# Padding of the low operand tile in the far SBUF pool: 40 elements instead of 8

## The chip, the cores and the metric

The kernel runs on one core of one Trainium2 chip. The metric is the device time of one execution in microseconds, as the median of several. Before the change three executions took 2014.45 to 2016.31 us, with a median of 2016.3 us.

## What is computed

One layer of an encoder trunk in float32, for one sequence of 256 tokens of width 2048. The normalised input goes through one wide projection that feeds three mixers (chunked attention, a diagonal state-space model called S5, and an mLSTM) and their gates; the gated sum is projected and added to the input; then come a cross-attention to 256 memory tokens and a gated feed-forward of width 5632:

```python
h = _rms(x, norm_mix[i])
qa, ka, va, us, xm, vm, om, im, fm, gpre = jnp.split(h @ w_in[i], splits, axis=-1)
...
merged = (gates[:, :, 0] * (ya @ w_br_a[i])
          + gates[:, :, 1] * (ys @ w_br_s[i])
          + gates[:, :, 2] * (ym @ w_br_m[i]))
x = x + merged @ w_out[i]
x = x + _mem_attention(_rms(x, norm_x[i]), mem_n, w_xq[i], w_xkv[i], g_xq[i], g_xk[i], w_xo[i])
x = x + _swiglu(_rms(x, norm_ffn[i]), w_gu[i], w_down[i])
```

## The kernel before

**Split products.** Every large product is made of three. Each float32 operand is split into a high part, rounded to the format that TensorE takes in one pass (`F32R`), and a low part, what is left. A product is high by high, plus high by low, plus low by high, added up in PSUM. `split_w` (lines 111 to 118) splits a weight block: ScalarE copies it into `whi` (line 116), VectorE subtracts into `wlo` (line 117). `split_act` (lines 203 to 210) does the same with an activation.

**The wide product, `gemm_i`** (lines 120 to 155). For 512 output columns it goes through the depth in tiles of 128 and through the two halves of the tokens. The activations, transposed so that depth lies along the partitions, are the stationary operand (128x128, loaded anew for each matmul); the weights stream past as the moving operand (128x512). There are three matmuls a step:

```python
PE.matmul(o, sh, h, start=(kt == 0), stop=False)              # line 146: high x whi
PE.matmul(o, sh, lw, start=False, stop=False)                 # line 147: high x wlo
PE.matmul(o, xl[:, kt, t * P:(t + 1) * P], h, start=False,    # line 148: low x whi
```

So a product of depth 2048 and 512 columns is 96 matmuls. `gemm_ii` (lines 157 to 175) is the other way about: the weights are stationary, the activations stream with 256 columns (lines 169 to 171).

**The operands.** An operand is a pair of tiles, high and low, of 16 depth tiles by 256 tokens, 16,384 bytes a partition each. Each stage writes the operand of the next: `to_operand` (lines 821 to 835) transposes four blocks on TensorE (line 827) and splits them. The stages that follow one another in time, with their stationary operands:

- the input projection: `xT` in poolA; within it the branch products with `ym`, `ya` and `ys` in p1, and the S5 gate, `gemm_ii` with `yg` in s5
- `w_out` (lines 880 to 889): `mT` in poolB, four products, 384 matmuls
- `w_xkv` (lines 915 to 937): `eT` in poolA, eight products, 768 matmuls
- `w_xq` (lines 946 to 997): `x1T` in poolB, four products, 384 matmuls, broken up by the attention of each head
- `w_xo` (lines 1001 to 1006): `oT` in poolA, 384 matmuls
- `w_gu` (lines 1016 to 1028): `x2T` in poolB, eleven rounds of a gate and an up product, 2112 matmuls, with eight transposes a round
- `w_down` (lines 1030 to 1039): `hT` in p3, four products of depth 5632, 1056 matmuls

**Where they lie.** The pools wp, poolA, p1 and s5 (later p2 and p3) are stacked upwards from the low end of SBUF, in the order in which they are opened. poolB and px1 are on the right side: poolB is stacked down from byte 229,344 of the partition and px1, with the residual `x1`, lies below it. Within a pool the tiles lie in the order of their first use. `mT`, `x1T` and `x2T` follow one another in the same two tiles of poolB. The byte offsets in a partition, worked out from the tiles' sizes and the allocator's order, before the change:

| tile | bytes from | modulo 256 |
|---|---|---|
| whi, wlo (four buffers each) | 36,672 to 65,344, every 4,096 | 64 |
| xT, eT, oT, high and low | 88,896 and 105,280 | 64 |
| hT, high and low | 88,896 and 133,952 | 64 |
| ya | 139,072 | 64 |
| ym, ys | 164,608 | 0 |
| yg | 198,528 | 128 |
| gt (two buffers) | 84,416 and 86,464 | 192 |
| part | 122,688 and on, every 4,096 | 64 |
| x1 | 180,160 | 192 |
| mT, x1T, x2T, high | 196,544 | 192 |
| mT, x1T, x2T, low | 212,928 | 192 |

All slices of an operand start at multiples of 512 bytes within it, so all lie at the same place modulo 256.

**What sets the order.** The scheduler orders the instructions by priority; weight loads and their splits come first (`WPRI`), PSUM evictions second (`EPRI`). Weights come in blocks of 1 MB through SyncE's queue (line 101), two buffers deep. The matmuls keep the order of the program, with transposes and the attention's small products put in between.

Of the kernel before, what the change touches and what calls it, by code (L numbers as in the profile page):

```python
# [10 lines left out]
F32R = mybir.dt.float32r  # L11
# [7 lines left out]
P = 128  # L19
T = 256  # L20
D = 2048
KD = D // P
# [30 lines left out]
def tile_block(ctx: ExitStack, tc: tile.TileContext, a: dict, out: bass.AP):  # L53
# [758 lines left out]
    poolB = tc.alloc_tile_pool(name="poolB", bufs=1, side="right")  # L812

    def operand_low(name):

        t = poolB.tile([P, KD * T + 8], F32R, tag="Bl", name=name)
        return t[:, 0:KD * T].rearrange("p (k t) -> p k t", t=T)
    mTh = poolB.tile([P, KD, T], F32R, tag="Bh", name="mT_h")
    mTl = operand_low("mT_l")

    def to_operand(srcs, dh, dl, k0, gname=None):
# [104 lines left out]

    fTh = poolB.tile([P, KD, T], F32R, tag="Bh", name="x1T_h")
    fTl = operand_low("x1T_l")
    for n in range(4):
        to_operand([x1[:, t, n * 512:(n + 1) * 512] for t in range(2)], fTh, fTl, 4 * n, "norm_x")  # L930
# [67 lines left out]

    gTh = poolB.tile([P, KD, T], F32R, tag="Bh", name="x2T_h")
    gTl = operand_low("x2T_l")  # L1000
    off = 0
    for n in range(4):
# [148 lines left out]
```

## Time and profile before

| | |
|---|---|
| profiled execution | 2013.28 us |
| its span | 2011.5 us |
| TensorE busy, matmuls | 2000.9 us, 9880 matmuls |
| TensorE busy, weight loads | 1670.1 us |
| VectorE busy | 1249.9 us |
| ScalarE busy | 975.0 us |
| GpSimd busy | 78.6 us |
| DMA | 377.78 MB, mean 188 GB/s |

The profile shows one execution. In a group of instructions by line the columns are the line, the engine, the operation, the output and the inputs by their names, the shape, the count, and then the busy time, the mean duration in ns and the idle time before. Matmuls overlap: each starts before the one ahead has ended, and their ends are modelled. So the pace of TensorE is the distance from one start to the next, which is read from the timeline (columns: start in us, duration in us, engine, line, operation, operands, count).

### The profile page before, as it was taken

The page shows a single profiled execution, that of the slowest core. Times are in us where ns is not written, and L with a number is a line of the kernel's source. Part 1 is how long each engine was busy: PE and PEld are TensorE (multiplying, and loading weights), DVE is VectorE, ACT ScalarE, POOL GpSimd, SP SyncE. Part 2 cuts the span into 40 slices and gives each one's busy share as a digit, 9 for nine tenths or more (in the row PEclk, how much of TensorE's full clock was granted, in tenths as well). Part 3 has the DMA queues.
Part 4 walks back from the last instruction along what each step waited for, and adds up shares of the span by engine and source line. Part 5 has one row for each costly group of instructions (what it writes and reads, how often), then busy time and mean ns, then how long its engine had stood idle before and what let it go on. Part 6 is the DMA issues. An engine that isn't in the chain of part 4 may idle for free.

```text
span 2011.5 us, 25145 instructions
## 1 busy us (share of the span) xinstructions
PE 2000.9 (99%) x9880; PEld 1670.1 (83%) x9880; DVE 1249.9 (62%) x1804; ACT 975.0 (48%) x1332; POOL 78.6 (4%) x142
## 2 busy tenths in 40 slices
PE   9999999999999999999999999999999999999999
PEld 7998888887887888888888888888888888888887
DVE  7967896669987857554545656554544444444443
ACT  7555556555444455555545545444444444433332
POOL 1001202000000000011000000000000000000000
PEclk9999999999999999999999999999999999999999
DMA  8555355555555656755454435555555555555553
GB/s 312 180 178 178 134 172 196 171 186 177 194 175 196 209 186 225 257 205 188 168 192 174 157 134 181 188 188 188 173 185 187 188 188 181 179 190 210 204 199 136
DMA packets 60406, 377.78 MB, mean 188 GB/s; under 512 B 6912, under 2 KB 8064, under 8 KB 18816
## 3 DMA queue, kind: packets, MB, share of 16 engines
q1 hardware_dynamic: 56880, 367.42, 52.0%
q0 software_dynamic: 2112, 6.82, 1.4%
q8 instruction: 77, 1.26, 0.3%
q10 hardware_dynamic: 1296, 1.95, 0.3%
q14 instruction: 41, 0.34, 0.0%
HBM read 374.06 MB, written 2.10 MB: 187 GB/s over the span
## 4 chain that ended last, share of the span: by engine, by line
PE 93%; DVE 4%; DMA 2%; ACT 0%; issue 0%; POOL 0%; SPq 0%; DVEq 0%; ACTq 0%
PE acc L147 27%; PE acc L146 27%; PE acc L148 27%; PE acc L170 2%; PE acc L169 2%; PE acc L171 2%; DVE wlo L117 2%; DMA raw<-in_w_in_dram 2%; PE sm L827 1%; PE sm L993 1%; PE sm L967 1%; PE sm L411 1%; ACT whi L116 0%; DVE s2k L442 0%; PE sm L911 0%
## 5 line engine op out<-in xcount | busy, mean ns | idle before, releaser
L117 DVE TENSOR_TENSOR wlo<-raw,whi 128x1024 fp32r<-128x1024 f32 (+2 forms) x700 | 833.9, 1193 | 668.2 <-ACT whi L116 665.0
L116 ACT CAST whi<-raw 128x1024 fp32r<-128x1024 f32 (+2 forms) x700 | 715.0, 1027 | 883.9 <-PE acc L148 677.1
L146 PE MATMUL acc<-whi,x2T_h 128*128 128x512 f32 x704 | 279.0, 396 | 0.0
L147 PE MATMUL acc<-wlo,x2T_h 128*128 128x512 f32 x704 | 278.9, 396 | 0.0
L148 PE MATMUL acc<-whi,x2T_l 128*128 128x512 f32 x704 | 278.0, 395 | 0.0
L147 PE MATMUL acc<-wlo,xT_h 128*128 128x512 f32 (+2 forms) x704 | 262.3, 373 | 1.8 <-DVE wlo L117 1.6
L148 PE MATMUL acc<-whi,xT_l 128*128 128x512 f32 (+2 forms) x704 | 261.1, 372 | 0.0
L146 PE MATMUL acc<-whi,xT_h 128*128 128x512 f32 (+2 forms) x704 | 259.7, 373 | 0.3 <-ACT whi L116 0.3
L148 PEld LDWEIGHTS acc<-whi,x2T_l 128*128 128x128 f32 x704 | 132.2, 188 | 31.7
L146 PEld LDWEIGHTS acc<-whi,x2T_h 128*128 128x128 f32 x704 | 132.2, 188 | 31.5
L147 PEld LDWEIGHTS acc<-wlo,x2T_h 128*128 128x128 f32 x704 | 132.2, 188 | 31.5
L147 PEld LDWEIGHTS acc<-wlo,xT_h 128*128 128x128 f32 x704 | 132.4, 188 | 27.3 <-DVE wlo L117 4.4
L146 PEld LDWEIGHTS acc<-whi,xT_h 128*128 128x128 f32 x704 | 131.8, 188 | 24.8 <-issue 1.3
L148 PEld LDWEIGHTS acc<-whi,xT_l 128*128 128x128 f32 x704 | 132.4, 188 | 23.3 <-issue 0.7
L147 PE MATMUL acc<-wlo,hT_h 128*128 128x512 f32 x352 | 137.0, 389 | 0.0
L146 PE MATMUL acc<-whi,hT_h 128*128 128x512 f32 x352 | 137.0, 389 | 0.0
L148 PE MATMUL acc<-whi,hT_l 128*128 128x512 f32 x352 | 136.9, 389 | 0.0
L169 PE MATMUL acc<-xT_h,whi 128*128 128x256 f32 x352 | 100.3, 285 | 2.1 <-DVE ev L627 2.1
L170 PE MATMUL acc<-xT_l,whi 128*128 128x256 f32 x352 | 100.7, 286 | 0.0
L148 PE MATMUL acc<-whi,eT_l 128*128 128x512 f32 x256 | 100.2, 391 | 0.0
L147 PE MATMUL acc<-wlo,eT_h 128*128 128x512 f32 x256 | 99.9, 390 | 0.0
L146 PE MATMUL acc<-whi,eT_h 128*128 128x512 f32 x256 | 99.8, 390 | 0.0
(376 smaller groups left out, 2832.3 us busy)
## 6 DMA issues: line engine op xcount, KB each, us to landing
raw<-in_w_gu_dram SPq DMA_DIRECT2D x88, 1024.0 KB, 4.7
raw<-in_w_in_dram SPq DMA_DIRECT2D x68, 1024.0 KB, 4.8
raw<-in_w_down_dram SPq DMA_DIRECT2D x44, 1024.0 KB, 4.7
raw<-in_w_xkv_dram SPq DMA_DIRECT2D x32, 1024.0 KB, 4.7
raw<-in_w_ii_dram SPq DMA_DIRECT2D x22, 1024.0 KB, 4.9
raw<-in_w_out_dram SPq DMA_DIRECT2D x16, 1024.0 KB, 5.0
raw<-in_w_xq_dram SPq DMA_DIRECT2D x16, 1024.0 KB, 4.7
raw<-in_w_xo_dram SPq DMA_DIRECT2D x16, 1024.0 KB, 4.7
```

Of the source, the lines that this page charges most:

```text
L116: S.copy(hi[:, :n], raw[:, c0:c1])
L117: V.tensor_tensor(lo[:, :n], raw[:, c0:c1], hi[:, :n].bitcast(F32), ALU.subtract)
L146: PE.matmul(o, sh, h, start=(kt == 0), stop=False)
L147: PE.matmul(o, sh, lw, start=False, stop=False)
L148: PE.matmul(o, xl[:, kt, t * P:(t + 1) * P], h, start=False, stop=(kt == nk - 1))
L169: PE.matmul(po, h, xh[:, kt, :], start=(kt == 0), stop=False)
L170: PE.matmul(po, h, xl[:, kt, :], start=False, stop=False)
L171: PE.matmul(po, lo[:, j * P:(j + 1) * P], xh[:, kt, :], start=False, stop=(kt == nk - 1))
L411: PE.matmul(pb[e][:, i * T:(i + 1) * T], bT[q:q + 32, i, c, :], u[q:q + 32, c, :], start=True, stop=True, tile_position=(q, 0))
L827: PE.transpose(px[:, j * T + t * P:j * T + (t + 1) * P], srcs[t][:, (kp + j) * P:(kp + j + 1) * P], ident)
L967: PE.matmul(pS[:, t * T:(t + 1) * T], qx[:, qi, d, t * P:(t + 1) * P], kx[:, ki, d], start=(d + i == 0), stop=(d == 3 and i == 2))
L993: PE.matmul(po[:, j * T:(j + 1) * T], vx[:, vi, m, c0:c0 + P], pT[pi][:, m * T:(m + 1) * T], start=(m + i == 0), stop=(m == 1 and i == 2))
```

## The change

One number, in the function that makes the low tile of an operand in poolB:

```diff
     def operand_low(name):
 
-        t = poolB.tile([P, KD * T + 8], F32R, tag="Bl", name=name)
+        t = poolB.tile([P, KD * T + 40], F32R, tag="Bl", name=name)
         return t[:, 0:KD * T].rearrange("p (k t) -> p k t", t=T)
     mTh = poolB.tile([P, KD, T], F32R, tag="Bh", name="mT_h")
     mTl = operand_low("mT_l")
```

The tile has KD x T = 4096 elements of four bytes and a padding that nothing reads or writes; the padding grows from 32 to 160 bytes. What is computed stays the same.

## The prediction

> **What bounds the kernel now.** I read the page first, then the chain of waits, then the matmuls one by one. On the page only the first lines matter.
>
> ```profile
> span 2011.5 us, 25145 instructions
> ...
> PE 2000.9 (99%) x9880; PEld 1670.1 (83%) x9880; DVE 1249.9 (62%) x1804; ACT 975.0 (48%) x1332; POOL 78.6 (4%) x142
> ...
> PE 93%; DVE 4%; DMA 2%; ACT 0%; issue 0%; POOL 0%; SPq 0%; DVEq 0%; ACTq 0%
> ```
>
> TensorE is busy all the time and is 93% of the chain that ends last. From 783 us to 2005 us, where all that the change touches lies, the chain by line names PE alone. What a matmul takes there is what the kernel takes. The chain, in order of time, gives a ruler for the gate and up stage: the six transposes of line 827 come once in each of its eleven rounds.
>
> ```profile
> 1269.93 0.65 PE sm L827 x6
> ...
> 1772.09 0.65 PE sm L827 x6
> ```
>
> So a round (192 matmuls and eight transposes) lasts (1772.09 - 1269.93) / 11 = 45.65 us.
>
> Now the matmuls. All that I compare are of the same form, 128x128 stationary against 128x512 moving, from lines 146 to 148. Busy means are no measure here, as each matmul begins before the last has ended. Their order in the groups by form is still telling:
>
> ```profile
> L146 PE MATMUL acc<-whi,x2T_h 128*128 128x512 f32 x704 | 279.0, 396 | 0.0
> ...
> L146 PE MATMUL acc<-whi,hT_h 128*128 128x512 f32 x352 | 137.0, 389 | 0.0
> ...
> L146 PE MATMUL acc<-whi,x1T_h 128*128 128x512 f32 x128 | 50.6, 395 | 0.0
> L146 PE MATMUL acc<-whi,mT_h 128*128 128x512 f32 x128 | 50.5, 395 | 0.0
> ...
> L146 PE MATMUL acc<-whi,oT_h 128*128 128x512 f32 x128 | 49.4, 392 | 0.0
> ```
>
> The three operands of the far pool (x2T, x1T, mT) stand at 395 and 396 ns, the others at 389 to 392. To get the true step I took the timeline of PE, with the starts of the first and the last matmul of a stretch, two rows for each operand, picked out of the answers for the windows in which they stand. The steps between them: x2T 190, hT 1033, mT 348, eT 121, x1T 121, ym 47, ya 47.
>
> ```profile
> 1270.34 0.47 PE L147 MATMUL acc<-wlo,x2T_h 128*128 128x512 f32 x1
> 1314.74 0.39 PE L148 MATMUL acc<-whi,x2T_l 128*128 128x512 f32 x1
> 1772.50 0.48 PE L147 MATMUL acc<-wlo,hT_h 128*128 128x512 f32 x1
> 2006.75 0.39 PE L148 MATMUL acc<-whi,hT_l 128*128 128x512 f32 x1
> 794.41 0.48 PE L148 MATMUL acc<-whi,mT_l 128*128 128x512 f32 x1
> 875.36 0.40 PE L148 MATMUL acc<-whi,mT_l 128*128 128x512 f32 x1
> 875.60 0.39 PE L146 MATMUL acc<-whi,eT_h 128*128 128x512 f32 x1
> 903.03 0.40 PE L147 MATMUL acc<-wlo,eT_h 128*128 128x512 f32 x1
> 1056.98 0.40 PE L146 MATMUL acc<-whi,x1T_h 128*128 128x512 f32 x1
> 1085.11 0.39 PE L147 MATMUL acc<-wlo,x1T_h 128*128 128x512 f32 x1
> 462.25 0.62 PE L146 MATMUL acc<-whi,ym 128*128 128x512 f32 x2
> 473.01 0.39 PE L148 MATMUL acc<-whi,ym 128*128 128x512 f32 x1
> 566.53 0.39 PE L146 MATMUL acc<-whi,ya 128*128 128x512 f32 x1
> 577.18 0.39 PE L148 MATMUL acc<-whi,ya 128*128 128x512 f32 x1
> ```
>
> Time over steps: eT 27.43 / 121 = 226.7 ns, ya 10.65 / 47 = 226.6, hT 234.25 / 1033 = 226.8; ym 10.76 / 47 = 228.9; x1T 28.13 / 121 = 232.5, mT 80.95 / 348 = 232.6, x2T 44.40 / 190 = 233.7. Put the addresses beside them. The moving operands whi and wlo always lie at 64 modulo 256. The stationary operands at 64 (eT, ya, hT, in three pools) step at 226.7; the one at 0 (ym) at 228.9; those at 192 (the far pool) at 232.5 to 233.7. One form, three phases, three paces; and the clock is the same, as the rows by stage further down show it at 1.00 for mT, x2T and hT alike.
>
> **The change, part by part.** Padding of 40 instead of 8 elements makes the low tile 16,544 bytes instead of 16,416. The pool is stacked down from byte 229,344, so the low tile goes from 212,928 to 212,800, the high tile from 196,544 to 196,416, and x1 below them from 180,160 to 180,032. All three go from 192 to 64 modulo 256. No instruction is added or removed, none is resized, and nothing is queued elsewhere.
>
> *Gate and up, 2112 matmuls on x2T.* The stretch of 44.40 us has 190 steps, the first of them long (it follows transposes; its row shows 0.47 us). The hT stretch begins the same way: 234.25 us less 1033 steps at eT's 226.69 ns leaves 0.08 us for that. At phase 64 the x2T stretch would take 190 x 0.22669 + 0.08 = 43.15 us: 1.25 us less, 6.58 ns a step. Over 2112 matmuls: 13.9 us. *w_out, 384 on mT.* 80.95 against 348 x 0.22669 + 0.08 = 78.97: 1.98 us, 5.7 ns a step; over 384: 2.2 us. *Cross-attention queries, 384 on x1T.* 28.13 against eT's 27.43 over 121 steps each: 5.8 ns; over 384: 2.2 us. Together 18.3 us.
>
> From this something comes off. After a break by other matmuls the pace has to settle again. The oT stage, at phase 64 but broken up by attention heads, shows 392 ns where hT shows 389: 3 ns a matmul. The x1T stage is broken up in the same way, so I take 384 x 3 ns = 1.1 us off: **17.2 us**. If mT pays this too, it is 18.3 - 2.3 = 16.0; if neither does, 18.3.
>
> Three edits come at nothing. x1 moves too: TensorE reads it in transposes alone, and these take the same 272 ns from x at 192 and from part at 64:
>
> ```profile
> L827 PE MATMUL sm<-cc,x 128*128 128x128 f32 x64 | 8.8, 272 | 0.0
> ...
> L827 PE MATMUL sm<-cc,part 128*128 128x128 f32 x32 | 4.6, 272 | 0.0
> ```
>
> The new lower edge of the pool lies within tiles of the S5 stage on which its old edge lay; the low tile now touches one more S5 scratch slot, for which the high tile waits already. And x1's edge stays 1,024 bytes above vx and hT_l, which end at 179,008. So no wait is added. If one were, it would hold up the splits of ACT and DVE into the operand, and the matmuls of w_out behind them, once.
>
> Does another engine become late when PE goes 3% faster? The stages of mT, x2T and hT side by side (time, then PE, PEld, DVE, ACT, POOL busy with counts, clock, DMA share, GB/s):
>
> ```profile
> 785.00:875.00 90.00, 90.00 (x393) 73.05 (x392) 53.75 (x64) 47.47 (x71) 3.98 (x8) 1.00 0.73 254
> 1264.00:1766.00 502.00, 502.00 (x2201) 405.08 (x2200) 244.67 (x225) 212.40 (x227) 1.46 (x4) 1.00 0.52 184
> 1767.00:2007.00 240.00, 240.00 (x1064) 198.60 (x1062) 110.49 (x97) 90.48 (x87) 0.00 (x0) 1.00 0.53 187
> ```
>
> The hT stage already runs the same weight loads and splits at the fast pace, with DVE and ACT under half busy and DMA at 0.53. The mT stage has DMA at 0.73, which becomes 0.75. Neither is a bound, so PE's time comes off the end one for one.
>
> The profiled execution took 2013.28 us, 1.8 over its span; less 17.2 that is 1996.1. It lies 3.0 us under the median of 2016.3 of the runs shown, so the median forecast is 2016.3 - 17.2 = **1999.1 us**.
>
> **A rule that speaks against it.** Rows first: same form, same clock, 226.7 ns at phase 64 and 233.7 at phase 192. The Trainium skill, "TensorE: Matmul & The Clock Gate", "Step-by-step: what each phase is for", says that TensorE has two independent read ports, and that loading the next weights takes no read bandwidth from the running matmul. By that rule an address could not matter and the sum would be 0, at 2016.3. The trace does not agree: something between the weight load and the stream depends on where they lie.
>
> **The rivals.** *The place, not the phase.* All three slow operands lie above byte 196,000, and no fast one of this form does. If the far end itself is slow, or the pool isn't stacked as I worked out, nothing changes: 2016.3. For it: place and phase can't be told apart for these three. Against it: ym is at 164,608, far below, and is off the fast pace too, at 228.9; hT runs at one pace over 90 KB of addresses; and yg, moving operand of the narrow matmuls, lies at 198,528 and is not slow (next rival). I give it 8%.
>
> *A middling pace.* mT and x2T lie at the same bytes, yet step at 232.6 and 233.7, so history has a hand in it. The new place might settle at ym's 228.9, 2.2 above the fast pace: (6.58 - 2.2) x 2112 + (5.75 - 2.2) x 768 = 9.3 + 2.7 = 12.0 us, 2004.3. Against it: eT, ya and hT all settle at the same value. 7%.
>
> *Like phases collide, so it gets slower.* In the narrow matmuls (lines 169 to 171, 256 columns, weights stationary at 64) it seems to be so. Two rows each, 251 and 107 steps:
>
> ```profile
> 60.43 0.36 PE L170 MATMUL acc<-xT_l,whi 128*128 128x256 f32 x1
> 90.63 0.28 PE L169 MATMUL acc<-xT_h,whi 128*128 128x256 f32 x1
> 737.10 0.28 PE L169 MATMUL acc<-yg,whi 128*128 128x256 f32 x1
> 749.71 0.28 PE L171 MATMUL acc<-yg,wlo 128*128 128x256 f32 x1
> ```
>
> With xT at 64, like the weights, a step takes 30.20 / 251 = 120.3 ns; with yg at 128, 12.61 / 107 = 117.9. Like phases cost 2.4 ns there. Were that so for wide matmuls at the far end, twice the columns would make it 4.9 ns, 14.1 us over 2880 matmuls: 2030.4. It decides if the wide pace at like phases is above 233.7. Against it stand eT, ya and hT, wide and alike, at 226.7. 3%.
>
> **How the numbers follow.** The forecast gets 82%, the rivals 8, 7 and 3%. A measurement of this kernel can tell about 0.2%, 4 us, from no change. The forecast and the middling pace are faster by more: 0.89; the place 0.08 same; collision 0.03 slower. The forecast's own bounds, savings of 16.0 to 18.3, give 1998.0 to 2000.3; the runs shown scatter from 2014.45 to 2016.31 and the profiled one is at 2013.28, so 3 us go under it: 1995.0. At the top the range reaches past the middling pace: 2005.0. Left out are the place and the collision and little else.
>
> **What would show it.** Right: in the profile after, starts on x2T, mT and x1T step at 226.7 to 227.5 ns; mean durations of x2T come down from 396 to about 389; a gate and up round on the chain lasts 45.65 - 192 x 6.58 ns = 44.4 us; PE stays at 99%. Wrong: steps still at 232 to 234 (the place), at 229 (middling), above 234 (collision); or the steps fall and PE waits for whi or wlo instead.

## The result and the profile after

The median went from 2015.64 us (four runs, 2014.45 to 2016.31) to 1997.24 us (four runs, 1997.08 to 1997.32): 18.4 us less, a ratio of 0.9909 with a 95% interval of 0.9892 to 0.9926. The profiled executions stand at 2013.28 and 1997.28 us, 16.0 apart. The instructions and their order on each engine are the same.

The page after the change, the same lines as before:

```profile
span 1995.5 us, 25145 instructions
...
PE 1984.5 (99%) x9880; PEld 1670.1 (84%) x9880; DVE 1249.9 (63%) x1804; ACT 976.4 (49%) x1332; POOL 77.8 (4%) x142
```

TensorE is still busy 99% of a span that is 16 us shorter, and its busy time has gone down by 16.4 us with the same 9880 matmuls. This is not a wait removed: the matmuls follow one another at a shorter distance. The ruler on the chain, the transposes that come once a round of gate and up:

```profile
1267.33 0.66 PE sm L827 x6
...
1756.06 0.66 PE sm L827 x6
```

A round lasts (1756.06 - 1267.33) / 11 = 44.43 us, against 45.65. The groups by form show which matmuls it was:

```profile
L146 PE MATMUL acc<-whi,x2T_h 128*128 128x512 f32 x704 | 274.9, 391 | 0.0
...
L146 PE MATMUL acc<-whi,hT_h 128*128 128x512 f32 x352 | 137.0, 389 | 0.0
...
L146 PE MATMUL acc<-whi,x1T_h 128*128 128x512 f32 x128 | 50.0, 391 | 0.0
...
L146 PE MATMUL acc<-whi,mT_h 128*128 128x512 f32 x128 | 49.8, 389 | 0.0
...
L146 PE MATMUL acc<-whi,oT_h 128*128 128x512 f32 x128 | 49.4, 392 | 0.0
```

x2T, x1T and mT have come from 395 and 396 ns to 389 to 391; hT and oT stand where they stood. The timeline of PE, first and last start of the same three stretches of the far pool:

```profile
1267.74 0.48 PE L147 MATMUL acc<-wlo,x2T_h 128*128 128x512 f32 x1
1310.93 0.39 PE L148 MATMUL acc<-whi,x2T_l 128*128 128x512 f32 x1
795.57 0.48 PE L148 MATMUL acc<-whi,mT_l 128*128 128x512 f32 x1
874.56 0.39 PE L148 MATMUL acc<-whi,mT_l 128*128 128x512 f32 x1
1056.16 0.39 PE L146 MATMUL acc<-whi,x1T_h 128*128 128x512 f32 x1
1083.59 0.39 PE L147 MATMUL acc<-wlo,x1T_h 128*128 128x512 f32 x1
```

x2T takes 43.19 us for 190 steps (227.3 ns, with the long first one), mT 78.99 for 348 (227.0), x1T 27.43 for 121 (226.7).

Where the time came from can be read off two markers that stand in both timelines, the start on mT in the first of its two rows and the last transposes before hT. Before, they are at 794.41 and 1772.09 us, 977.68 apart; after, at 795.57 and 1756.06, 960.49 apart. The stages of the far pool and what lies between them gave 17.19 us. The other 1.2 us of the profiled difference go the other way and arise before the first marker. This is scatter: the first matmul on mT starts at 785.5 us before and at 786.8 after, and at 788.6 in a later execution of the same kernel as after (`after_again` below).

### The profile page after: what moved, and what is told of

It reads as the page before. It is cut to its first block, busy times and chain, and to the rows that moved or that the text cites. A ratio compares the mean times of both kernels' runs of the same rounds, so it can differ in the third digit from the quotient of the medians.

```text
span 1995.5 us, 25145 instructions
## 1 busy us (share of the span) xinstructions
PE 1984.5 (99%) x9880; PEld 1670.1 (84%) x9880; DVE 1249.9 (63%) x1804; ACT 976.4 (49%) x1332; POOL 77.8 (4%) x142
## 4 chain that ended last, share of the span: by engine, by line
PE 97%; DVE 1%; DMA 1%; issue 0%; ACT 0%; SPq 0%; POOL 0%; DVEq 0%; ACTq 0%
PE acc L147 28%; PE acc L146 28%; PE acc L148 28%; PE acc L170 2%; PE acc L169 2%; PE acc L171 2%; PE sm L827 1%; DMA raw<-in_w_in_dram 1%; PE sm L411 1%; PE sm L993 1%; PE sm L967 1%; DVE wlo L117 0%; PE sm L911 0%; PE sm L215 0%; PE sm L456 0%
## 5 line engine op out<-in xcount | busy, mean ns | idle before, releaser
L147 PE MATMUL acc<-wlo,x2T_h 128*128 128x512 f32 x704 | 274.9, 391 | 0.0
L146 PE MATMUL acc<-whi,x2T_h 128*128 128x512 f32 x704 | 274.9, 391 | 0.0
L148 PE MATMUL acc<-whi,x2T_l 128*128 128x512 f32 x704 | 273.9, 389 | 0.0
```

The costliest lines, as they stand in the source:

```text
L148: PE.matmul(o, xl[:, kt, t * P:(t + 1) * P], h, start=False, stop=(kt == nk - 1))
```

## The experiments

Four theories stood against each other. A: the distance modulo 256 between the stationary operand and the weights that stream past it sets the pace. B: the far end of SBUF is slow. C: 192 modulo 256 is a bad place in itself. D: the accesses of the other engines or the DMAs collide with TensorE's.

**Place or phase.** The edit:

```diff
-        t = poolB.tile([P, KD * T + 8], F32R, tag="Bl", name=name)
+        t = poolB.tile([P, KD * T + 72], F32R, tag="Bl", name=name)
```

> The change with a padding of 72 elements instead of 40: the far pool lies 128 bytes lower still, but at 192 modulo 256 as before the change. If the phase between the stationary operand and the weights decides (theory A), the steps on mT, x1T and x2T go back to 232 to 234 ns and the time to 2013 to 2016 us. If moving away from the far end helped (theory B, the place), they stay at 226.7 to 227.5 ns and the time at 1997.

The median was 2015.47 us, the ratio to before 1.0 (0.9991 to 1.001). The timeline of this kernel, the stretch on x2T:

```profile
1271.67 0.47 PE L147 MATMUL acc<-wlo,x2T_h 128*128 128x512 f32 x1
1316.07 0.39 PE L148 MATMUL acc<-whi,x2T_l 128*128 128x512 f32 x1
```

44.40 us for 190 steps, to the hundredth what it was before. The pool was moved further than in the change and gained nothing. B falls.

**Distance or absolute place.** Everything on the left side is moved up by 128 bytes; a scratch tile is halved to make room:

```diff
-        t = scr.tile([P, 512], BF16, tag=tag, name=nm(tag), bufs=1)
+        t = scr.tile([P, 256 if tag == "jkm" else 512], BF16, tag=tag, name=nm(tag), bufs=1)
...
-    mhalf = const.tile([P, 4], F32, name="mhalf")
+    mhalf = const.tile([P, 36], F32, name="mhalf")
```

> The kernel before, with everything but the far pool moved up by 128 bytes: the weights, poolA, p1 and p3 lie at 192 modulo 256 like the far pool, which stays where it was. If the distance between stationary and moving operand decides (A), all wide matmuls with both at 192 step at 226.7 ns and the time is 1997 us. If 192 is a bad place for a stationary operand in itself (theory C), the other 4464 wide matmuls slow down by 6 ns too and the time is 2016 + 27 = 2043 us. If the far end is slow (B), nothing changes: 2013 to 2016.

The median was 1998.06 us, the ratio 0.9921 (0.9904 to 0.9937), and the timeline shows x2T and hT:

```profile
1268.33 0.48 PE L147 MATMUL acc<-wlo,x2T_h 128*128 128x512 f32 x1
1311.53 0.39 PE L148 MATMUL acc<-whi,x2T_l 128*128 128x512 f32 x1
1757.25 0.47 PE L147 MATMUL acc<-wlo,hT_h 128*128 128x512 f32 x1
1991.52 0.39 PE L148 MATMUL acc<-whi,hT_l 128*128 128x512 f32 x1
```

43.20 / 190 = 227.4 and 234.27 / 1033 = 226.8 ns. The far pool was not touched here, yet it sped up as by the change: the weights came to it. C falls, and B once more.

**High and low apart.** Both tiles get room for a shift, and each half its own, in elements of four bytes (the edit against the kernel before):

```diff
-    def operand_low(name):
...
-        t = poolB.tile([P, KD * T + 8], F32R, tag="Bl", name=name)
-        return t[:, 0:KD * T].rearrange("p (k t) -> p k t", t=T)
...
+    def operand(tag, name, o):
...
+        t = poolB.tile([P, KD * T + (64 if tag == "Bh" else 104)], F32R, tag=tag, name=name)
+        return t[:, o:o + KD * T].rearrange("p (k t) -> p k t", t=T)
+    mTh = operand("Bh", "mT_h", 0)
+    mTl = operand("Bl", "mT_l", 32)
...
+    fTh = operand("Bh", "x1T_h", 32)
+    fTl = operand("Bl", "x1T_l", 0)
```

> The change, with the halves of two operands shifted inside their tiles: mT high at 64 and low at 192, x1T high at 192 and low at 64, x2T both at 64. Two of three weight loads are of the high half. If each load pays for itself (A, loads apart), mT steps at 226.7 + 1.9 = 228.6 ns, x1T at 226.7 + 3.9 = 230.6, x2T at 226.7, and the time is 1997 + 0.7 + 1.5 = 1999 us. If one load out of phase puts the whole cycle out, both step at 232 to 233 and the time is 2001. By B nothing changes from 1997.

One run took 2002.26 us. The timeline:

```profile
796.99 0.47 PE L148 MATMUL acc<-whi,mT_l 128*128 128x512 f32 x1
877.49 0.40 PE L148 MATMUL acc<-whi,mT_l 128*128 128x512 f32 x1
1059.11 0.40 PE L146 MATMUL acc<-whi,x1T_h 128*128 128x512 f32 x1
1087.36 0.39 PE L147 MATMUL acc<-wlo,x1T_h 128*128 128x512 f32 x1
```

mT, with one load of three off, steps at 80.50 / 348 = 231.3 ns, x1T, with two of three off, at 28.25 / 121 = 233.5, more than the 232.5 that it had with all three off. So the loads don't each pay for themselves. In the steady part of the mT stretch the step from line 146 to 147 takes 226.7 ns, that from 147 to 148 takes 232.5 and that from 148 to the next 146 takes 234.2: with one load of three off, two steps of three are long. Both versions of A missed: the first by far, the second by less than 1 ns a step and 1.3 us in the time.

**TensorE alone.** In the gate and up stage of the kernel before, only the first block of weights is loaded and split; the other blocks are left out, and all matmuls of the stage read the first one's split weights:

```diff
-            if first is None:
+            if keep:
+                pass
+            elif first is None:
                 raw = load_w(blk, kk * n)
...
-                hi, lo = split_w(raw, k2 * n, (k2 + step) * n)
+                if not keep:
+                    made = split_w(raw, k2 * n, (k2 + step) * n)
+                    if keep is not None:
+                        keep.append(made)
+                hi, lo = keep[0] if keep else made
```

> The kernel before, with the weight blocks of the gate and up stage left out but the first: its 2112 matmuls all read the same split weights, so that in this stage VectorE, ScalarE and the DMAs do nothing but evictions, transposes and splits of h (the output is that of wrong weights). If the loss is between TensorE's own weight loads and stream (A), x2T steps at 229 and 238 in turn, 233.3 on average, and the time is 2013 to 2016 us. If the writes of the splits or the DMAs collide with TensorE's reads (theory D), the step falls to 227 or below and the time to 2002 or less.

One run took 2012.69 us. A window of 30 us in this stage (time, busy times with counts, clock, DMA share, GB/s), and two stretches of 65 steps:

```profile
1280.00:1310.00 30.00, 30.00 (x131) 24.11 (x130) 0.70 (x1) 2.55 (x3) 0.00 (x0) 1.00 0.00 1
```

```profile
1318.29 0.39 PE L152 MATMUL acc<-whi,x2T_h 128*128 128x512 f32 x1
1333.45 0.40 PE L154 MATMUL acc<-whi,x2T_l 128*128 128x512 f32 x1
1728.07 0.39 PE L152 MATMUL acc<-whi,x2T_h 128*128 128x512 f32 x1
1743.17 0.39 PE L154 MATMUL acc<-whi,x2T_l 128*128 128x512 f32 x1
```

VectorE works 0.7 us of 30, ScalarE 2.55, the DMA share is 0.00, and the steps take 15.16 / 65 = 233.2 and 15.10 / 65 = 232.3 ns. The whole stage on x2T takes 500.93 us, 1.3 less than the 502.24 before, where the change takes off 13.5. D falls: the loss is there with TensorE almost alone. The two paces show that the same addresses carry more than one pattern.

**The whole curve, wide.** In the kernel after, the weights are shifted inside their buffers, by another 16 bytes in each of the 22 gate and up products, and split in twice as many pieces of half the length to leave room:

```diff
-        hi = wp.tile([P, 1024], F32R, tag="whi", name=nm("whi"), bufs=4)
-        lo = wp.tile([P, 1024], F32R, tag="wlo", name=nm("wlo"), bufs=4)
+        hi = wp.tile([P, 1024], F32R, tag="whi", name=nm("whi"), bufs=4)[:, o:]
+        lo = wp.tile([P, 1024], F32R, tag="wlo", name=nm("wlo"), bufs=4)[:, o:]
...
-            step = 1 if first is not None and k == 0 else 2
+            step = 1 if o is not None or first is not None and k == 0 else 2
...
+        off = gemm_i(gTh, gTl, KD, a["w_gu"], off, 512, evg, o=8 * n % 64)
+        off = gemm_i(gTh, gTl, KD, a["w_gu"], off, 512, evu, o=(8 * n + 4) % 64)
```

> The kernel after the change, where the split weights of the 22 gate and up products lie a bit further up in their buffers in each: by 0, 16, 32 bytes and so on up to 240, then 0 to 80 again (the splits are made half as long, twice as many, to leave room). The stationary operand stays at 64. If the distance between the two modulo 256 sets the pace (A), it is 226.7 ns at 0, about 229 at 64 (as ym has it, weights 64 above the operand), 232 to 234 at 128, and the products 16 to 21 repeat the paces of 0 to 5. If only whole steps of 64 count, 16 to 48 stand at 226.7 like 0. Time 2000 to 2010 us.

One run took 2011.57 us. The mean of the last 65 steps of each product, from the starts in the timeline, by the bytes that the weights lie above the operand (modulo 256):

| above | ns | above | ns | above | ns | above | ns |
|---|---|---|---|---|---|---|---|
| 0 | 226.7 | 64 | 228.9 | 128 | 232.3 | 192 | 233.3 |
| 16 | 231.6 | 80 | 231.1 | 144 | 233.3 | 208 | 234.7 |
| 32 | 233.3 | 96 | 233.4 | 160 | 234.2 | 224 | 233.3 |
| 48 | 233.4 | 112 | 231.0 | 176 | 233.3 | 240 | 233.3 |

The timeline rows behind the entries 0 and 64, from their second pass:

```profile
1637.04 0.39 PE L146 MATMUL acc<-whi,x2T_h 128*128 128x512 f32 x1
1651.78 0.39 PE L148 MATMUL acc<-whi,x2T_l 128*128 128x512 f32 x1
1727.67 0.39 PE L146 MATMUL acc<-whi,x2T_h 128*128 128x512 f32 x1
1742.56 0.39 PE L148 MATMUL acc<-whi,x2T_l 128*128 128x512 f32 x1
```

14.74 / 65 and 14.89 / 65, from starts that are rounded to 0.01 us: 226.8 and 229.1. All six repeated distances came out within 0.05 ns of the first pass. There is one good place, sharp to 16 bytes, a half good one at 64, and the rest lies between 231.0 and 234.7. The entry at 64 is what ym had (228.9), the one at 128 what mT had (clean steps without the first, 232.4). But x2T before the change lay at 128 too and stepped at 233.4: away from the good place a distance can carry more than one pace, and with one or two products at each the table is good to about 1 ns there, by this one case. The excess of the 22 products, each times its 96 matmuls, adds up to 11.1 us. The rest of the 14.3 us over the kernel after lies ahead of this stage, which begins 3.4 us later.

**The whole curve, narrow.** The same shift for the 22 narrow products of the input projection, where the weights are stationary (splits of 6, 6 and 4 depth tiles, `kk = min(6, nk - k)`, and `o` of 0, 4, 8 and so on elements).

> The kernel after the change, where in the 22 narrow products of the input projection (weights stationary, xT moving) the split weights lie further up by 16 bytes more in each product, 0 to 240 and again from 0 to 80 (three splits of 6, 6 and 4 depth tiles instead of two of 8). From the rows of the kernel before: 120 ns at 0; 116.3 at 64 (as for mqk, where the moving operand lies 64 below the weights); 117.9 at 192 (as for yg, 64 above). In between unknown; A expects a smooth or stepped curve with the period of 256 bytes, and the highest value near 0, the other way about than in the wide matmuls. Time 1994 to 1998 us.

One run took 1994.9 us. The mean of the steps in a product (those between two matmuls of the stage, without the interrupted ones), by the bytes of the weights above xT: 119.9 ns at 0, 118.4 at 16, 117.7 at 32, 117.8 at 48, **114.2** at 64, then 118.7 to 119.9 from 80 to 160, and 116.7 to 118.1 from 176 to 240. The second pass gave 119.6, 118.4, 118.3, 117.9, 113.5 and 118.7. So in this scan the narrow matmuls have their best place at 64, and equal phases are among their worst. The next kernels show how far that carries.

**Putting it to use.** A kernel that puts the narrow weights 64 above xT (the argument 16, in elements, at all three calls), one that also puts the other split products at their best distance, and the change once more, on one chip:

```diff
+        gemm_ii(xAh, xAl, KD, w_ii, (6 + i) * NII, xm_evac(i), None, 16)
...
+        off = gemm_i(xAh, xAl, KD, w_in, off, MD + (8 if h == 0 else 0), vm_evac(h),
+                     None, 48)
...
+            at["v"] = p1.tile([P, 2064], F32, tag="V", name="va")[:, 0:2048]
...
+        qx = p2.tile([P, 8 * T + 64], F32R, tag="qx", name=nm("qx"))[:, 16:16 + 8 * T]
+        vx = p2.tile([P, 4 * XD + 16], F32R, tag="vx", name=nm("vx"))[:, 16:]
```

> The kernel after the change, with the split weights of all 22 narrow products of the input projection 64 bytes above the phase of xT (three splits of 6, 6 and 4 depth tiles instead of two of 8). By A and the scan (120.0 at 0, 113.5 to 114.2 at 64) 1056 narrow matmuls save 6 ns each: 6.3 us, to 1991 us. If the narrow gain of the scan is eaten by waits for the additional splits, 1994 to 1997.

> As narrow64, and every other product of split operands put at its best distance too: ym and ys moved from 0 to 64 (336 wide matmuls, 2.3 ns less each: 0.8 us), the weights of vm at 0 with xT at 64 (384 matmuls of 256 or 264 columns, some 6 ns less: 2.3 us), the weights of the S5 gate 64 above yg (108, 3.8 ns: 0.4 us), qx and vx of the cross-attention 64 above what streams past them (192, 5 ns: 1.0 us). By A it is 4.5 us under narrow64: 1986.5 us. If the distances matter in the large weight products alone, it is at 1991 like narrow64.

> The kernel after the change once more, unaltered, for the comparison on the same chip: 1997 to 1998 us, and closer from run to run than the kernel before.

| kernel | median us | lowest to highest | ratio to before |
|---|---|---|---|
| after_again | 1998.36 | 1997.46 to 1999.08 | 0.9914 (0.9899 to 0.9928) |
| narrow64 | 1995.97 | 1993.67 to 1996.49 | 0.9898 (0.9882 to 0.9915) |
| tuned | 1991.43 | 1991.03 to 1992.80 | 0.9881 (0.9866 to 0.9895) |

The change run again kept within 1.6 us, the kernel before beside it within 4.3 (2013.16 to 2017.45). narrow64 gave 2.4 us instead of 6.3. Only part of its products ran at the fast pace: the clean steps of a product average 113.3 ns in some and 117.8 in others, at the same distance. Over all 22 products they average 114.8 ns, against 119.8 in the change run again, which is worth 5.2 us. And TensorE now waits where it did not. The stretch from 60 to 200 us, first in the change run again, then in narrow64:

```profile
60.00:200.00 140.00, 139.73 (x1070) 134.05 (x1070) 108.72 (x258) 75.14 (x124) 9.77 (x14) 1.00 0.52 176
```

```profile
60.00:200.00 140.00, 136.81 (x1059) 131.25 (x1058) 107.77 (x263) 75.00 (x130) 7.81 (x12) 0.99 0.52 176
```

TensorE is idle 0.27 us of the one and 3.19 of the other. The waits of narrow64 between 60 and 270 us name the splits (line waiting, line waited for: total, times, longest):

```profile
PE acc L169 <- ACT whi L116: 1.4, 2, 1.1
...
PE acc L171 <- DVE wlo L117: 0.6, 1, 0.6
```

Between 200 and 270 us it is the other way about, 2.64 us idle in the change run again and 0.77 in narrow64, so that over the 785 us ahead of the far pool narrow64 waits 1.3 us more (8.77 against 7.47). Both profiled executions also have one short stretch in which the granted clock fell. First narrow64, then the change run again:

```profile
96.00:108.00 12.00, 11.51 (x83) 11.31 (x84) 7.86 (x15) 7.49 (x13) 0.00 (x0) 0.86 0.24 79
240.00:252.00 12.00, 10.61 (x81) 9.51 (x82) 11.22 (x27) 5.66 (x10) 0.00 (x0) 0.86 0.25 90
```

Some 16 narrow steps in a row take 213 to 214 ns there instead of 113 or 120, about 1.6 us more in the one and 1.4 in the other, so this all but cancels between the two. The remaining 1.5 us or so of the 5.2 were not taken apart.

tuned is 4.5 us under narrow64, as forecast from it, and 6.9 under the change: its slowest run, 1992.80 us, is below the fastest of either. But the sum was right with wrong parts, which is luck. The 108 matmuls on yg stayed at 117.8 ns with their weights 64 above, where 114 was expected. The clean steps on vm went from 120.2 to 118.7 ns, 0.6 us of the 2.3 forecast. The stages on x1T and oT, through which the cross-attention runs, became 0.5 us shorter together, of 1.0 forecast. The steps on ym and ys came down, as they should, to 226.7 where nothing broke them, which gave 0.6 us of 0.8. These are 1.7 us of the 4.5. The profiled executions are 3.7 us apart, and the stretch at the lower clock, which tuned does not have, makes up an estimated 1.6 us of that.

## Why the prediction was right, point by point

*The bound.* TensorE sets the end, and its time comes off one for one: its busy time fell by 16.4 us, the span by 16.0. No other engine became late in the stages of the far pool: in the windows after the change TensorE is busy all of the 90 us from 785 on and all of the 489 us from 1261 on.

*The cause.* The far pool was slow because of its phase against the weights. It was argued from three phases and three paces, with place and phase confounded for the far pool. lower256 and all192 took them apart. The rule of the Trainium skill that was weighed against it ("TensorE: Matmul & The Clock Gate", "Step-by-step: what each phase is for": loading the next weights takes no read bandwidth from the running matmul), and by which an address could not matter, does not agree with these runs: the loss is there with the other engines nearly at rest (232.3 and 233.2 ns), and in the scan the pace goes from 226.7 to 234.7 ns with the distance of the two alone.

*The sum.* The three stretches were forecast at 43.15, 78.97 and 27.43 us and measured 43.19, 78.99 and 27.43. The total of 17.2, made of 18.3 less 1.1 for settling, stands against 17.19 between the two markers. That it fits to a hundredth is luck, as the parts show below. The median forecast, 1999.1, was 1.9 us too high: with a fourth run the median before stood at 2015.64 instead of 2016.3, and the medians fell by 18.4 us, 1.2 more than came off between the two markers. That is within the scatter of the runs before, some 4 us (2013.44 to 2017.21 in thirteen later ones).

*What was mis-sized.* The settling was put on the x1T stage alone. It is there (391 ns on x1T where mT has 389), but x2T pays some too, at 391 where hT has 389; forecast was "about 389" for it. Taken from the first matmul on one operand to the first on the next, the stage of mT went from 90.11 to 87.98 us, that of x1T from 107.08 to 105.37 and that of x2T from 502.24 to 488.73: 2.1, 1.7 and 13.5 us less, where 2.2, 1.1 and 13.9 were forecast. So x1T lost half of what was taken off for it, x2T lost 0.4 that was not, and the two errors cancel.

*The rivals.* "The place" fell with lower256. "Like phases collide" was right for the narrow matmuls and wrong for the wide ones. "A middling pace" did not come about, but its argument holds: one distance can carry two paces, 232.3 and 233.2 on x2T in the kernel with TensorE alone, 113.3 and 117.8 in narrow64.

What stays open is what in the memory makes the distance matter. The runs show that it repeats with 256 bytes (lower256), that it acts between TensorE's own two operands, and that one load in three brings most of the loss (231.3 ns on mT in halves, between 226.7 and 232.6). They do not show which parts of the memory are in each other's way.

## What to carry to other kernels

When TensorE is busy all the time, compare its pace from start to start between stages that run the same form; busy shares and waits show nothing of such a loss. If two stages differ, put the addresses of both operands modulo 256 beside the paces, and move one of them with a padding. Scan the distance by form before choosing, and look at the pace again afterwards: for 512 moving columns the best one was 0 in the scan, and it held in the other kernels here; for 256 it was 64 in the scan, but that gave the fast pace in part of the products alone. Three quarters of the gain in a step can hang on 16 bytes.

## What the runs showed that was not expected

The good place is narrow: 16 bytes off cost 4.9 of the 6.6 ns, 32 bytes all of it. The patterns are exact and stable: on x2T before the change the steps alternate between 229 and 238 ns for a whole round, and on mT, at the same addresses, seven steps repeat, the longest 241. Which one sets in is decided in the first steps after a break: in the kernels before and alone, a stretch on x2T or mT that starts with a step of 313 to 315 ns goes on to alternate, one that starts with 317 to 321 goes on with the seven. What brings about the one or the other is not shown. And the order of good and bad distances turns over with the number of moving columns: at equal phases 512 columns take their shortest step, 226.7 ns, and 256 columns one of their longest, 120.
